# Two weight blocks at a time in the experts' job that mixes two kinds of matmul pass

## The chip, the cores and the metric

One core of a Trainium2 chip runs the whole program. The metric is the device time in microseconds, from launch to end, taken over several runs. The profile is one execution of the same program, recorded by the hardware profiler.

## What is computed

Two layers of a hybrid backbone over 256 latent tokens and 256 context tokens, model width 1024, in float32. Each layer normalises and modulates the stream, projects it into four parallel mixers (pooling, short convolution, neighbourhood attention, state space), projects back, and then applies a feed-forward block. In layer 0 that block is a dense SwiGLU; in layer 1 it is a mixture of experts, and the change touches only that:

```python
logits = (h @ w_router).astype(jnp.float32)
top_v, top_i = lax.top_k(logits, TOP_K)               # 2 of 8 experts for each token
gates = jax.nn.softmax(top_v, axis=-1)
for e in range(N_EXPERTS):
    w_e = jnp.sum(jnp.where(top_i == e, gates, 0.0), axis=-1).astype(h.dtype)
    out = out + w_e[..., None] * swiglu(h, w_gu[e], w_down[e])
# swiglu: g, u = split(h @ w_gu, 2); (silu(g) * u) @ w_down
# w_gu[e] is 1024 x 2816, w_down[e] is 1408 x 1024
```

All weights of all experts are read from device memory once, 138 MB out of the 262 MB that the program reads.

## The kernel before

The kernel is written with a tile framework. Its planner simulates the program and writes out an order of instructions for each engine; each engine then runs its own list strictly in that order, with semaphores between engines. `inorder` adds a dependency without a semaphore: it only tells the planner that one instruction has to stand behind another in the list of the same engine.

**Experts by number of tokens.** The experts are sorted on the chip by how many tokens chose them, so expert 0 is the longest. Each gets a fixed number of token slots. Slots are packed into passes of 128 slots. A *split* pass (128 slots of one expert) multiplies at reduced-precision speed, form `128*128`: ScalarE copies a raw weight block into a high part `wh` (line 284), VectorE subtracts to get the low part `wl` (line 287), and TensorE does three products for each slice of 128 inputs: high by `wh`, high by `wl`, low by `wh`. A *whole* pass multiplies the raw float32 block directly, in quarters of 32 slots, form `128*32`, four of them side by side; it needs no split. Its 128 slots may belong to several experts.

**Jobs.** `moe` runs four jobs one after the other and spreads a fifth one, the last job, between their steps:

- job of expert 0: one pass of a special whole kind, which has its own code (`products2`);
- job of expert 2: one split pass;
- job of experts 1 and 4: a split pass of expert 1 (128 slots), and a whole pass (32 slots of expert 1 and 96 of expert 4). This is the job with two kinds of pass;
- job of expert 3: one split pass;
- the last job, experts 5, 6 and 7: one whole pass. `LAST` names the steps of the other jobs after which one step of it is run. Eleven of these, and one double one, lie in the job of experts 1 and 4; its down half runs at the end of the program.

**One job** (`expert`). The up half has six output blocks `nt`, each of 256 gate and 256 up columns (the sixth has 128 and 128). For each output block the weights come in four blocks of 512 KB for each expert, with two slices `k` of 128 inputs in each; the sixth has two blocks with four slices. For each block, `blocks` loads one raw slot for each expert and splits it if a split pass wants it, and then `products` is called for each pass and each slice. Products accumulate in one PSUM bank for each pass. At the end of an output block comes the gated activation: a tanh on ScalarE, two operations on VectorE (lines 1662 to 1664), and transposes on TensorE (line 1563). The down half has eleven blocks `f` of 512 KB, and each is multiplied for both halves `h` of the output. A job yields after every two blocks, and that is a step: eleven in the up half and five in the down half.

**Buffers.** The raw slots form a ring, which is filled in program order by one DMA queue (SyncE, lines 308 and 323): 15 slots in this stage by the trace, two of them in the tile `xres`. A load waits until the slot's previous block is released. `wh` and `wl` have three buffers each (`NSPLIT`).

**Order of TensorE.** `products` ties each run of a whole pass to the run before it that used the same set of blocks, through `ws["turn"]`. It also notes the latest product of any job in `self.mgu`. Split products are tied to nothing; they run when their `wh` and `wl` are there and the planner puts them there.

Of the kernel before, what the change touches and what calls it, by code (L numbers as in the profile page):

```python
# [247 lines left out]
class Piece:  # L248
# [3 lines left out]
    def __init__(self, col, n, expert, whole, half=None):  # L252
        self.col, self.row, self.n, self.expert, self.whole, self.half = col, col % P, n, expert, whole, half


class Kern:
# [1281 lines left out]
    def expert(self, eids, passes, ys, last=False):  # L1538
# [21 lines left out]
        def trans(pieces, h, j, n):  # L1560
            p = self.ps("m", "atr")
            for i in range(n):
                E.transpose(p[:, i * P:i * P + P], h[:, i * P:i * P + P], self.cst("ident"))
            src = p[:, :n * P].rearrange("p (f s) -> p f s", f=n)
            if pieces[0].whole:
                A.copy(w[:, 0, 2 * j:2 * j + n], src)
                return
            a, = (c.a for c in pieces)
            A.copy(a[:, 0, 2 * j:2 * j + n], src)
            V.tensor_tensor(a[:, 1, 2 * j:2 * j + n], src, a[:, 0, 2 * j:2 * j + n].bitcast(F32), op=OP.subtract)  # L1570

        def trans_sum(p, j, n):

            t = self.tmp("mth")[:, :2 * n * P]
            A.copy(t, p[:, :2 * n * P])
            s = self.stack.shape[-1]
            q = self.ps("m", "atr")
            for i in range(2 * n):
                self.mm(q[:, i * s:i * s + s], t[:, i * P:i * P + P], self.stack)
            gate, up = (q[:, i * n * s:i * n * s + n * s] for i in range(2))  # L1580
            th = self.tmp("mth")[:, :n * s]
            A.activation(th, gate, AF.Tanh, scale=0.5)
            V.scalar_tensor_tensor(th, th, 1.0, gate, op0=OP.add, op1=OP.mult)
            th, up = (v.rearrange("p (f s) -> p f s", f=n) for v in (th, up))
            self.glu = V.scalar_tensor_tensor(w[:, 0, 2 * j:2 * j + n], th, 0.5, up, op0=OP.mult, op1=OP.mult)

        def blocks(gu, *at):
            ws = {}
            for e in eids:
                if gu and self.w0:  # L1590
                    ws[e] = self.w0.pop(0), None
                    continue
                nt, b = at
                if gu:
                    ap = a["mg0"][self.eid[e], nt, b] if nt < 5 else a["mg1"][self.eid[e], b]
                    n, parts = 1024, 1
                elif last:
                    n = min(2, 11 - nt)
                    ap = a["md"][self.eid[e], nt:nt + n, :, b * 512:b * 512 + 512].rearrange("f p c -> p f c")
                    n, parts = n * 512, n  # L1600
                else:
                    ap, n, parts = a["md"][self.eid[e], nt], 1024, 1
                r = self.raw(ap, n, parts, split=parts == 1 or e not in whole)
                ws[e] = r, self.split(r) if e in split else None
            return ws

        def product(out, c, x, w, s, start, stop):
            if c.whole:
                r = w[0]
                if len(r.shape) == 3:  # L1610
                    r, out = r[:, s.start // 256:s.stop // 256], self.quarters(out)
                else:
                    r = r[:, s]
                return [self.mm(out[c.row + q:c.row + q + QUART], x[:, 0, q:q + QUART], r, start=start, stop=stop)
                        for q in range(0, c.n, QUART)]
            wh, wl = (t[:, s] for t in w[1])
            return [self.mm(out, x[:, 0], wh, start=start, stop=False),
                    self.mm(out, x[:, 0], wl, start=False, stop=False),
                    self.mm(out, x[:, 1], wh, start=False, stop=stop)]

        def products(out, pieces, get, ws, s, start, stop):


            ms = [m for c in reversed(pieces) for m in product(out, c, get(c), ws[c.expert], s, start, stop)]
            if pieces[0].whole:
                self.inorder(ws.setdefault("turn", [])[-1:] + ms)
                ws["turn"] = ms
            self.mgu = ms[-1]

        turn = []  # L1630

        def products2(todo):

            ms = [m for t in todo for m in product(*t)]
            self.inorder(turn[-1:] + ms)
            turn[:] = ms
            self.mgu = ms[-1]

        for nt in range(6):
            hw = 256 if nt < 5 else P  # L1640
            kb = 2 if nt < 5 else 4
            ps = [self.ps("g", "mgu") for _ in passes]
            for b in range(8 // kb):
                ws = blocks(True, nt, b)
                for p, (pieces, _) in zip(ps, passes):
                    if half:
                        products2([(p[:, :2 * hw], pieces[kk % 2], pieces[0].x[:, :, b * kb + kk],
                                    ws[pieces[0].expert], slice(kk * 2 * hw, kk * 2 * hw + 2 * hw), b * kb + kk < 2, b * kb + kk > 5)
                                   for kk in range(kb)])
                        continue  # L1650
                    for kk in range(kb):
                        k = b * kb + kk
                        products(p[:, :2 * hw], pieces, lambda c: c.x[:, :, k], ws,
                                 slice(kk * 2 * hw, kk * 2 * hw + 2 * hw), k == 0, k == 7)
                if (last or b % 2) and b < 8 // kb - 1:
                    yield
            for p, (pieces, _) in zip(ps, passes):
                if half:
                    trans_sum(p, nt, hw // P)
                    continue  # L1660
                th = self.tmp("mth")[:, :hw]
                A.activation(th, p[:, :hw], AF.Tanh, scale=0.5)  # L1662
                V.scalar_tensor_tensor(th, th, 1.0, p[:, :hw], op0=OP.add, op1=OP.mult)  # L1663
                self.glu = V.scalar_tensor_tensor(th, th, 0.5, p[:, hw:2 * hw], op0=OP.mult, op1=OP.mult)
                trans(pieces, th, nt, hw // P)
            yield
# [10 lines left out]
        if last:  # L1677
            pieces, gate = passes[0]
            ys += [mp.tile([P, 2, 512], F32R, tag="ymoe", name="ylast", bufs=2),
                   mp.tile([P, 512], F32, tag="aT", name="ylast1", bufs=1)]  # L1680
            for h in range(2):
                p = self.ps("g", "mdn")
                for f in range(11):
                    if f % 2 == 0:
                        ws = blocks(False, f, h)
# [3 lines left out]
                for q in range(2):  # L1689
                    s = slice(q * 256, q * 256 + 256)  # L1690
# [5 lines left out]
                yield  # L1696
            return
        py = [[self.ps("g", "mdn") for h in range(2)] for _ in passes]
        for f in range(11):
            if half:  # L1700
                ws = [blocks(False, f, 0)] if f % 2 == 0 else ws + [blocks(False, f, 0)]
                if f % 2 == 0 and f < 10:
                    continue
                pieces = passes[0][0]
                e = pieces[0].expert
                products2([(py[0][h], pieces[g % 2 if f < 10 else h], pieces[0].a[:, :, g], ws[g % 2][e],
                            slice(h * 512, h * 512 + 512), g < 2, g in ((9, 10), (8, 10))[h])
                           for h in range(2) for g in ((f - 1, f) if f < 10 else (f,))])
                if f % 2:
                    yield  # L1710
                continue
            ws = blocks(False, f, 0)
            for pys, (pieces, _) in zip(py, passes):
                for h in range(2):
                    products(pys[h], pieces, lambda c: c.a[:, :, f], ws, slice(h * 512, h * 512 + 512), f == 0, f == 10)
            if f % 2:
                yield
        for pys, (_, gate) in zip(py, passes):
# [305 lines left out]
```

## Time and profile before

| | us |
|---|---|
| median of 3 runs | 1214.59 (1214.19 to 1215.19) |
| profiled execution, its own time | 1213.07 |
| span of the profile, first to last instruction | 1211.3 |

| engine | busy, us | share of the span |
|---|---|---|
| TensorE, products (PE) | 1165.6 | 96% |
| TensorE, weight loads (PEld) | 831.0 | 69% |
| VectorE (DVE) | 736.8 | 61% |
| ScalarE (ACT) | 461.1 | 38% |

The experts' stage runs from about 830 us to 1200 us of the span. The job of experts 1 and 4 takes about 943 to 1098 us, the job of expert 3 from there to about 1160. In the timeline a product is named by its output and what it reads: `mgu` and `mdn` are the PSUM tiles of the up and down halves, `xg` the tokens of a split pass, `xgv` those of the whole pass of experts 4 and 1, `xgw` those of the last job; `aT`, `aTv` and `aTw` are the same for the down half. A float32 product of form `128*32` is recorded as two instructions, so one block of a whole pass (two slices of four quarters) shows as 16. Products are pipelined and their durations overlap: the distance between two starts is what counts. Shares of the load engines are averages over 16 engines and can read slightly above 1.

### The profile page before, as it was taken

To read this page: it belongs to the slowest core of one execution; us is meant where nothing else is said; L and a number is where in the kernel's file an instruction comes from. 1 tells how busy PE (TensorE), PEld (TensorE's weight loads), DVE (VectorE), ACT (ScalarE), POOL (GpSimd) and SP (SyncE) were. 2 spreads that over 40 slices of the span, in tenths; PEclk is the share of its full clock that TensorE was granted. 3 is DMA by queue.
4 is the path that set the end of the run, shared out by engine and by line. 5 is a ranking of instruction groups with operands and counts; after the bars stand their busy time and mean duration, and the time that the engine had idled before them with its cause. 6 is when DMAs were issued, how large, how long until landed. Compare 5 with 4: busy or idle time off the path is not lost. (4 is left out here: it accounts for less than half of the span.)

```text
span 1211.3 us, 17942 instructions
## 1 busy us (share of the span) xinstructions
PE 1165.6 (96%) x6601; PEld 831.0 (69%) x6601; DVE 736.8 (61%) x1612; ACT 461.1 (38%) x863; POOL 8.9 (1%) x30
## 2 busy tenths in 40 slices
PE   6999999999999999999999999988999999999994
PEld 3787676787788888888886897884467534446741
DVE  4554667347979756764336778644588524447942
ACT  4443453324322231232223555541276423435721
POOL 0000000000000000000000000000000000000000
PEclk9999999999999999999999999998999999999997
DMA  9635424229565443543223442276999999896984
GB/s 373 228 138 209 144 83 139 84 87 374 201 206 187 162 155 128 187 154 122 87 101 126 141 139 88 90 252 244 359 401 407 344 401 394 300 409 238 375 286 179
DMA packets 88752, 264.16 MB, mean 218 GB/s; under 512 B 8144, under 2 KB 24144, under 8 KB 88528
## 3 DMA queue, kind: packets, MB, share of 16 engines
q1 hardware_dynamic: 88080, 260.84, 59.1%
q0 software_dynamic: 576, 2.10, 0.5%
q8 instruction: 54, 0.88, 0.3%
q14 instruction: 42, 0.34, 0.1%
HBM read 261.85 MB, written 1.05 MB: 217 GB/s over the span
## 5 line engine op out<-in xcount | busy, mean ns | idle before, releaser
L287 DVE TENSOR_TENSOR wl<-raw,wh 128x512 fp32r<-128x512 f32 (+2 forms) x288 | 257.0, 920 | 108.9 <-ACT wh L284 108.0
L284 ACT ACTIVATE wh<-raw 128x512 fp32r<-128x512 f32 (+2 forms) x288 | 225.4, 815 | 250.6 <-PE dps L342 67.3
L342 PE MATMUL g<-hmix,wh 128*128 128x512 f32 (+1 forms) x640 | 182.3, 364 | 0.3
L342 PEld LDWEIGHTS g<-hmix,wh 128*128 128x128 f32 x640 | 112.3, 189 | 31.6 <-issue 11.3
L342 PE MATMUL gps<-hffn,wh 128*128 128x512 f32 x320 | 125.0, 394 | 0.8 <-DVE gth L1158 0.8
L342 PE MATMUL ups<-hffn,wh 128*128 128x512 f32 x320 | 124.8, 394 | 0.0
L342 PE MATMUL g<-hmix,wl 128*128 128x512 f32 (+1 forms) x320 | 114.9, 359 | 0.0
L342 PE MATMUL dps<-aT,wh 128*128 128x512 f32 x352 | 111.0, 394 | 0.0
L453 DVE SCALAR_TENSOR_TENSOR sprod<-raw,srep 128x1024 f32<-128x1024 f32 x72 | 87.8, 1220 | 26.3 <-DMA raw<-in_adat_dram 25.8
L342 PE MATMUL mgu<-wh,xg 128*128 128x512 f32 (+1 forms) x288 | 89.2, 381 | 0.0
L342 PEld LDWEIGHTS dps<-aT,wh 128*128 128x128 f32 x352 | 66.0, 188 | 15.8
L342 PEld LDWEIGHTS gps<-hffn,wh 128*128 128x128 f32 x320 | 60.4, 189 | 15.4 <-DVE gth L1158 1.2
L342 PEld LDWEIGHTS ups<-hffn,wh 128*128 128x128 f32 x320 | 60.5, 189 | 14.2
L342 PE MATMUL dps<-aT,wl 128*128 128x512 f32 x176 | 69.7, 396 | 0.0
L342 PEld LDWEIGHTS g<-hmix,wl 128*128 128x128 f32 x320 | 60.4, 189 | 8.4 <-issue 1.0
L342 PE MATMUL ups<-hffn,wl 128*128 128x512 f32 x160 | 63.4, 396 | 0.0
L342 PE MATMUL gps<-hffn,wl 128*128 128x512 f32 x160 | 63.4, 396 | 0.0
L342 PEld LDWEIGHTS mgu<-wh,xg 128*128 128x128 f32 x288 | 52.8, 188 | 13.1 <-issue 3.8
L342 PE MATMUL mgu<-wl,xg 128*128 128x512 f32 (+1 forms) x144 | 57.4, 398 | 0.0
L1138 DVE SCALAR_TENSOR_TENSOR xres<-dps,mods,xres 128x256 f32<-128x256 f32 x64 | 27.5, 477 | 28.6 <-PE dps L342 28.4
L1663 DVE SCALAR_TENSOR_TENSOR mth<-mth,mgu 128x256 f32<-128x256 f32 (+1 forms) x30 | 11.5, 394 | 53.2 <-ACT mth L1662 52.8
L342 PE MATMUL mdn<-wh,aT 128*128 128x512 f32 x132 | 43.5, 400 | 0.0
(396 smaller groups left out, 1820.1 us busy)
## 6 DMA issues: line engine op xcount, KB each, us to landing
raw<-in_mg_dram SPq DMA_DIRECT2D x141, 512.0 KB, 6.7
raw<-in_md_dram SPq DMA_DIRECT2D x76, 512.0 KB, 7.5
raw<-in_ada_dram SPq DMA_DIRECT2D x60, 512.0 KB, 4.1
raw<-in_fg_dram SPq DMA_DIRECT2D x44, 512.0 KB, 4.2
raw<-in_wi_dram SPq DMA_DIRECT2D x40, 512.0 KB, 4.3
raw<-in_adat_dram SPq DMA_DIRECT2D x36, 512.0 KB, 3.3
xres<-in_mg_dram SPq DMA_DIRECT2D x23, 512.0 KB, 7.5
raw<-in_fd_dram SPq DMA_DIRECT2D x22, 512.0 KB, 3.3
```

The source lines that it names most:

```text
L284: up = self.A.activation(h, src, AF.Copy)
L287: sub = self.V.tensor_tensor(lo, src, h.bitcast(F32), op=OP.subtract)
L342: return self.E.matmul(out, l, r, start=start, stop=stop, skip_group_check=True)
L453: V.scalar_tensor_tensor(y, t[:, :1024], 1.0, s[:, j], op0=OP.mult, op1=OP.mult, accum_out=o[:, q, j:j + 1])
L1138: self.V.scalar_tensor_tensor(self.x[:, d, s], ps[:, s], gt[:, j:j + 1], self.x[:, d, s], op0=OP.mult, op1=OP.add)
L1663: V.scalar_tensor_tensor(th, th, 1.0, p[:, :hw], op0=OP.add, op1=OP.mult)
```

## The change

In a job with more than one pass, weight blocks are loaded and split as before, but the products wait for two blocks: first all slices of both blocks for the split pass, then all of both for the whole pass. The same is done in the down half, where the eleventh block is alone. Jobs with one pass keep their order. In addition, a run of a whole pass is no longer tied to the run before it with the same blocks but to the latest product of any job (`self.mgu`), in all jobs that have such runs, the last job included.

```diff
             ms = [m for c in reversed(pieces) for m in product(out, c, get(c), ws[c.expert], s, start, stop)]
             if pieces[0].whole:
-                self.inorder(ws.setdefault("turn", [])[-1:] + ms)
-                ws["turn"] = ms
+                self.inorder([self.mgu] + ms)
             self.mgu = ms[-1]
...
             ps = [self.ps("g", "mgu") for _ in passes]
+            wss = []
             for b in range(8 // kb):
                 ws = blocks(True, nt, b)
-                for p, (pieces, _) in zip(ps, passes):
+                if len(passes) > 1:
+
+                    wss.append(ws)
+                    if b % 2 == 0:
+                        continue
+                    for p, (pieces, _) in zip(ps, passes):
+                        for k in range((b - 1) * kb, (b + 1) * kb):
+                            s = slice(k % kb * 2 * hw, k % kb * 2 * hw + 2 * hw)
+                            products(p[:, :2 * hw], pieces, lambda c: c.x[:, :, k], wss[k // kb], s, k == 0, k == 7)
+                for p, (pieces, _) in zip(ps, passes if len(passes) == 1 else ()):
                     if half:
...
         py = [[self.ps("g", "mdn") for h in range(2)] for _ in passes]
+        wss = []
         for f in range(11):
...
-            ws = blocks(False, f, 0)
+            wss.append(blocks(False, f, 0))
+            if len(passes) > 1 and f % 2 == 0 and f < 10:
+                continue
             for pys, (pieces, _) in zip(py, passes):
-                for h in range(2):
-                    products(pys[h], pieces, lambda c: c.a[:, :, f], ws, slice(h * 512, h * 512 + 512), f == 0, f == 10)
+                for g in range(f - 1 if len(passes) > 1 and f < 10 else f, f + 1):
+                    for h in range(2):
+                        products(pys[h], pieces, lambda c: c.a[:, :, g], wss[g], slice(h * 512, h * 512 + 512), g == 0,
+                                 g == 10)
             if f % 2:
                 yield
```

## Rows read from the trace of the kernel before

**Rows 1.** Chain that ended last, in order of time: start us, us, what.

```profile
1172.47 6.46 DMA raw<-in_md_dram
...
1180.76 10.69 DMA raw<-in_md_dram
```

**Rows 2.** Stages: length; PE, PEld, DVE, ACT, POOL busy (count); clock, DMA share, GB/s.

```profile
943.00:1030.00 87.00, 87.00 (x602) 36.99 (x605) 35.12 (x74) 26.96 (x61) 0.00 (x0) 1.00 1.00 378
1030.00:1098.00 68.00, 68.00 (x463) 28.68 (x455) 29.71 (x56) 26.10 (x54) 0.00 (x0) 1.00 0.92 344
1098.00:1160.00 62.00, 60.03 (x352) 44.46 (x352) 52.63 (x104) 39.44 (x79) 0.00 (x0) 1.00 0.83 297
1160.00:1211.00 51.00, 32.71 (x228) 13.85 (x228) 14.02 (x39) 9.59 (x25) 0.00 (x0) 0.88 0.66 238
```

**Rows 3.** The same columns for two slices of 10 us.

```profile
950.00:960.00 10.00, 10.00 (x72) 4.92 (x74) 4.06 (x8) 1.63 (x3) 0.00 (x0) 1.00 0.77 261
...
1060.00:1070.00 10.00, 10.00 (x67) 4.14 (x66) 5.06 (x8) 3.81 (x7) 0.00 (x0) 1.00 1.03 416
```

**Rows 4.** PE's timeline, experts 1 and 4: start us, us, engine, line, out<-in, form, count.

```profile
942.99 1.92 PE L342 MATMUL mgu<-raw,xgv 128*32 128x512 f32 x16
944.84 0.51 PE L342 MATMUL mgu<-wl,xg 128*128 128x512 f32 x1
...
971.58 1.92 PE L342 MATMUL mgu<-raw,xgw 128*32 128x512 f32 x16
...
1002.57 1.93 PE L342 MATMUL mgu<-xres,xgv 128*32 128x512 f32 x16
1004.43 0.50 PE L342 MATMUL mgu<-wl,xg 128*128 128x512 f32 x1
...
1005.99 1.92 PE L342 MATMUL mgu<-raw,xgv 128*32 128x512 f32 x16
1007.85 0.50 PE L342 MATMUL mgu<-wl,xg 128*128 128x512 f32 x1
...
1008.50 1.92 PE L342 MATMUL mgu<-raw,xgw 128*32 128x512 f32 x16
1010.35 0.50 PE L342 MATMUL mgu<-wh,xg 128*128 128x512 f32 x1
...
1039.36 1.48 PE L342 MATMUL mgu<-raw,xgv 128*32 128x512 f32 x9
...
1042.91 0.44 PE L1563 MATMUL atr<-constp,mth 128*128 128x128 f32 x2
...
1096.92 1.06 PE L342 MATMUL mdn<-rawo,aTv 128*32 128x512 f32 x6
```

**Rows 5.** Waits from 940 to 1060: total us, times, longest us.

```profile
SPq L323 <- PE mgu L342: 56.2, 30, 5.3
...
PEld mgu L342 <- DMA raw<-in_mg_dram: 3.3, 9, 0.4
```

**Rows 6.** One issue on the sync queue; issues by tile, median us to landing, 960 to 1030.

```profile
983.56 2.95 SPq L308 DMA_DIRECT2D xres<-in_mg_dram  x2
...
xres<-in_mg_dram SPq DMA_DIRECT2D x8, 512.0 KB, 7.0
```

**Rows 7.** ACT's timeline at the end of an output block; in brackets idle time before.

```profile
999.20 0.66 ACT L1662 ACTIVATE mth<-mgu 128x256 f32<-128x256 f32 x2 [9.92 <-PE mgu L342]
999.74 1.15 ACT L284 ACTIVATE wh<-xres 128x512 fp32r<-128x512 f32 x2
```

**Rows 8.** Groups of lines, 943 to 1098: busy us, mean ns, idle before.

```profile
L287 DVE TENSOR_TENSOR wl<-raw,wh 128x512 fp32r<-128x512 f32 x55 | 35.3, 686 | 19.6 <-ACT wh L284 19.5
...
L284 ACT ACTIVATE wh<-raw 128x512 fp32r<-128x512 f32 x55 | 31.3, 626 | 16.7 <-PE mdn L342 15.0 <-PE mgu L342 1.8
```

**Rows 9.** Job of expert 3: a wait on PE's timeline; waits from 1100 to 1165.

```profile
1142.70 0.50 PE L342 MATMUL mdn<-wl,aT 128*128 128x512 f32 x1 [1.65 <-DVE wl L287]
...
SPq L323 <- DVE wl L287: 21.6, 13, 4.6
```

## The prediction

> **What bounds the kernel now.** I read the chain of waits first: the program ends on the last expert job's down weights, with two stretches of transfer of 6.46 and 10.69 us in its last 40 us [rows 1]. So what counts is how early the queue of weight loads gets there, and that queue is paced by buffers. Next I read busy time by stage [rows 2]. From 943 to 1098 us runs the job with two kinds of pass (experts 1 and 4). TensorE is busy for all 155 us there, VectorE for 35.12 of 87 and 29.71 of 68. From 1098 to 1160 (expert 3, one split pass) VectorE takes over with 52.63 of 62. In the first of these, the sync queue waits 56.2 us for TensorE to release a weight buffer, while no wait of a weight load of TensorE for a transfer exceeds 0.4 us [rows 5]. A slot loaded at 983.56 takes 7.0 us to land [rows 6] and is multiplied at 1002.57 [rows 4], so it lies ready for some 12 us. I conclude that TensorE's own order sets the pace from 943 to 1098, with transfers close behind: 378 and 344 GB/s in the two halves, where a 10 us slice reaches 416 [rows 2, 3].
>
> **What the change removes.** TensorE's timeline [rows 4] alternates between products of form 128\*128 (split pass) and 128\*32 (whole passes: xgv of this job, xgw of the last job). I price one alternation from its rows. Split stretches: six products from 1004.43 to 1005.99 take 1.56 us, two from 1007.85 to 1008.50 take 0.65; so one costs (1.56-0.65)/4 = 0.23, and a stretch costs 0.65-2\*0.23 = 0.19 besides. Whole stretches: one block's run takes 1.85 us (1008.50 to 1010.35); two runs that happen to be adjacent, 1039.36 to 1042.91, take 3.55, which is 2\*1.85-3.55 = 0.15 less. So an alternation costs 0.34, say 0.35 us.
>
> Their number: from 942.99 to 1096.92 I count 52 stretches of form 128\*32 (the first and last stand in [rows 4]). By the code 33 are blocks of this job's own whole pass (20 + 2 up, 11 down), 12 are blocks of the last job, the rest are runs cut in two. After: 11 up steps with one double run each, and 5 + 1 in the down pass, so 17. The last job's run is now tied behind the latest product, which is the double run's last: it lands next to it, and costs no alternation of its own. At the six ends of an output block the transposes (128\*128) will probably stand between the two, 6 more: 23. Bounds: 17 if all are adjacent, 28 if every last-job run stands alone. Gain (52-23)\*0.35 = 10.2 us, bounds 8.4 and 12.3. No product, load or split is added, and the order of the loads is the same: each step still loads the same blocks in the same turn.
>
> **What it adds: a split pass that needs two split blocks at once.** Three buffers of wh/wl exist. When a pair's split pass begins, its two and the next one are full; the first is released halfway. From there ScalarE and VectorE have the rest of that pass (0.7 us) and the whole runs behind it (3.55 us alone, some 5.2 with the last job's) to refill two. A block costs VectorE 2\*0.686 = 1.37 us and ScalarE 2\*0.626 = 1.25 [rows 8]: 2.7 against 4.2 or more. Inside an output block, and in the down pass, I take 0. At the end of an output block ScalarE's queue is in the way: the tanh of both passes stands ahead of the next split (tanh at 999.20, split at 999.74, [rows 7]), and with it all that is queued behind. Now the tanh of the split pass can run beside the whole run, and only that of the whole pass waits; then follow split 1 (1.25), two copies and split 2. TensorE has the last job's run of 1.85 to cover that, and 1.4 us of the first block's products. I reckon up to 0.7 us open at each of 5 ends, and take 0.2: 1 us, bounds 0 and 3.5.
>
> **At the start of the job** the whole run at 942.99 covered the wait until the first wl at 944.84 [rows 4]. It can't go first any more; the products of the scatter can partly fill in. I take 1 us of the 1.85, bounds 0 and 1.9.
>
> **What stays at nothing, and its cover.** The raw slots of a pair are held until the double run, later than now by up to half a step, and seven are released within some 4 us instead of spread over 9. The cover is the 12 us for which a slot lies ready. A step now takes (1008.50-971.58)/4 = 9.2 us [rows 4] for 7 loads of 0.524 MB, 398 GB/s. With two alternations less it takes 8.5 us, 432 GB/s, which is above 416: the transfers fall behind by 7\*0.524/416 = 8.8 less 8.5, 0.3 us a step, or 3 us in ten steps (6 us at 400 GB/s). That comes out of the 12. From 1030 to 1098 the load engines have 8% free, and before 960 more (261 GB/s) [rows 2, 3], so they catch up. If that cover were gone, the second rival below would hold. The last job's whole runs in the jobs of experts 2 and 3 also lose their freedom: six runs of 1.85 us in stages which VectorE paces; I take 0, bounds -1 and +1.
>
> The Trainium skill would set the ceiling lower. DMA: Bandwidth & Descriptors, "Specifications", states an HBM limit of about 358 GB/s per core. By that rule this stage is at its limit, and the gain is nil. The trace disagrees: 416 GB/s over 10 us [rows 3], and the measurement decides.
>
> **Where the gain goes.** What TensorE saves by 1098 lets the next job begin as much earlier. That job is VectorE's; its queue of loads waits 21.6 us for VectorE's splits [rows 9], and the load engines are used at 0.83, so it keeps its length and moves as a whole. The tail's loads follow from its releases; 297 and 238 GB/s in the two last stages leave room. So the end moves by the whole sum: -10.2+1+1 = -8.2 us. The profiled execution took 1213.07 us (span 1211.3) and becomes 1204.9. The median of the runs is 1.5 us above it, at 1214.59: I predict 1206.5 us. The likeliest case's own range is 1202.5 (12.3 saved, nothing given back) to 1210.5 (8.4 saved, 4.5 given back).
>
> **Rivals.**
> *The transfers bind.* For it: a share of 1.00 in 943 to 1030, and a slot held longer in a ring. Against: 12 us of stock. Then TensorE saves nothing up to 1030, and later at most the 8% of 68 us, 5.4; I reckon half to all of it, 1209 to 1212: 1211 us.
> *The runs don't come together.* The tie only says "after"; the planner that orders each engine may still put the next pair's split products inside a double run or ahead of the last job's run, as it now cuts whole runs in pieces (45 planned, 52 seen). Then some 40 alternations remain: 12\*0.35 = 4.2, less 1 to 2: 1212 us.
> *TensorE starves for splits* (the slower side). Place: the second split block of each of the 17 pairs, with ScalarE's queue held by a tanh or by a wh buffer that TensorE hasn't released. Price: up to a block's 1.37 us each. In the next job such a wait for a wl shows once, 1.65 us [rows 9]. It decides from 10.2/17 = 0.6 us a pair: above that the change loses. At 1.37 it is 17\*1.37 = 23.3 less 10.2: 13 us slower, 1228; at 0.8 it is 1218. Against it: 2.7 us of work in 4.2 or more.
>
> **How the numbers follow.** Forecast 0.58, transfers 0.15, runs apart 0.12, starving 0.15. About 0.2%, 2.4 us, is what a measurement of this kernel can tell from no change: 1212.2 to 1217.0. Faster: all of the forecast, most of the transfers' case and a third of the runs' case, 0.74. The same: what is left of these two and the mildest fifth of starving, 0.14. Slower: 0.12. The range 1202.0 to 1214.5 holds the forecast and the first two rivals, and leaves out the starving and a sliver below.
>
> **What would show it.** In the job's timeline: 17 to 28 stretches of form 128\*32, whole runs of four or six products' rows length (3.55 or 5.2 us), a step of 8.5 us, no idle time ahead of wl products beyond 1 us, and the stage of expert 3 beginning near 1090 instead of 1098. The chain's end would look the same, 8 us earlier. I am wrong if stretches stay above 35, if TensorE shows gaps that end on VectorE's wl or on a transfer of a microsecond or more at most pairs, or if expert 3 begins earlier and the end does not.

## The result, and the profile after

The changed kernel takes 1202.87 us (median of 4 runs, 1199.97 to 1205.38), the kernel before beside it 1214.89 us: a ratio of 0.9898 [0.9877, 0.9918] (the 95% interval stands in brackets here and below), 12.0 us less. On another chip it was 1203.01 against 1214.42, 0.9893 [0.9875, 0.9911]. The profiled execution of the changed kernel took 1202.79 us (span 1201.0), 10.3 us less than that of the kernel before, which had been 1.8 us under its median.

The chain that ended last, in order of time (start us, us, what), after:

```profile
1161.73 6.38 DMA raw<-in_md_dram
1170.06 10.69 DMA raw<-in_md_dram
1180.80 4.57 PE mdn L342 x24
```

The end is the same as in [rows 1]: the last two stretches of transfer, one of 10.69 us again, about 10.7 us earlier. To place the gain I cut both traces at the same events: first split product of experts 1 and 4, first of expert 3, end of expert 3's last wl split, start of the last run (24 recorded instructions of form 128\*32). The columns are those of [rows 2]. Before:

```profile
942.70:1098.70 156.00, 156.00 (x1063) 66.39 (x1062) 65.83 (x129) 54.06 (x116) 0.00 (x0) 1.00 0.96 363
1098.70:1156.70 58.00, 56.04 (x328) 42.67 (x326) 51.91 (x103) 38.30 (x77) 0.00 (x0) 1.00 0.82 296
1156.70:1191.50 34.80, 29.53 (x219) 12.61 (x217) 7.82 (x18) 5.69 (x12) 0.00 (x0) 1.00 0.95 341
```

After:

```profile
943.90:1090.50 146.60, 146.04 (x1066) 69.92 (x1064) 66.21 (x129) 55.36 (x117) 0.00 (x0) 1.00 1.00 379
1090.50:1147.80 57.30, 56.59 (x330) 43.30 (x329) 52.04 (x103) 38.72 (x76) 0.00 (x0) 1.00 0.88 325
1147.80:1180.80 33.00, 28.66 (x219) 12.59 (x217) 7.81 (x18) 5.58 (x12) 0.00 (x0) 1.00 0.98 357
```

In finer numbers: the job starts 1.3 us later (943.93 against 942.66) and takes 146.57 us instead of 156.06 (-9.5), expert 3's job 57.31 instead of 58.01 (-0.7), the tail 32.99 instead of 34.77 (-1.8). With 0.4 us more behind the last run this makes the 10.3 us. The later start is not the work of the new order: 1.3 us are lost already 30 us into the program, where the order on the engines is the same. A second profiled execution of the changed kernel has a job of 146.54 us again, but a tail of 34.01, so a single tail length is good to about a microsecond only. The number of products in a stage and the work of VectorE and ScalarE are the same but for a missing record or two; TensorE does the same job in less busy time.

TensorE's timeline of a step and an end of output block, after, columns as in [rows 4]:

```profile
992.82 0.50 PE L342 MATMUL mgu<-wh,xg 128*128 128x512 f32 x1
...
995.78 3.64 PE L342 MATMUL mgu<-raw,xgv 128*32 128x512 f32 x32
999.35 0.44 PE L1563 MATMUL atr<-constp,mth 128*128 128x128 f32 x2
999.72 1.92 PE L342 MATMUL mgu<-raw,xgw 128*32 128x512 f32 x16
1001.57 0.50 PE L342 MATMUL mgu<-wh,xg 128*128 128x512 f32 x1
...
1004.00 0.50 PE L342 MATMUL mgu<-wl,xg 128*128 128x512 f32 x1 [0.23 <-DVE wl L287]
...
1005.36 1.92 PE L342 MATMUL mgu<-xres,xgv 128*32 128x512 f32 x16
1007.10 1.90 PE L342 MATMUL mgu<-raw,xgv 128*32 128x512 f32 x16
1008.82 1.90 PE L342 MATMUL mgu<-raw,xgw 128*32 128x512 f32 x16
1010.65 0.50 PE L342 MATMUL mgu<-wh,xg 128*128 128x512 f32 x1
```

The whole runs now stand together: two blocks (995.78 to 999.35) or two and the last job's (1005.36 to 1010.65, 5.29 us), with twelve split products ahead (992.82 to 995.78, 2.96 us). A step of two blocks is 2.96 + 5.29 = 8.25 us where it was 9.2. At the end of an output block the transposes come between, as forecast. I count 26 stretches of form 128\*32 in the job, where there were 52.

Waits in the job, after (total us, times, longest us; the sync queue up to 1055, the others up to 1090), and one issue on the sync queue:

```profile
SPq L323 <- PE mgu L342: 49.2, 26, 7.0
...
PE mgu L342 <- DVE wl L287: 0.5, 2, 0.2
...
PEld mgu L342 <- DMA raw<-in_mg_dram: 2.1, 7, 0.4
PEld mdn L342 <- DMA raw<-in_md_dram: 1.3, 4, 0.4
...
ACT wh L284 <- DMA raw<-in_mg_dram: 1.5, 2, 1.1
...
984.94 5.12 SPq L308 DMA_DIRECT2D xres<-in_mg_dram  x2
```

No wait of TensorE for a transfer exceeds 0.4 us, as in [rows 5]; ScalarE's splits wait for one twice, 1.1 us at most. The two loads of the last row, issued at 984.94 and 989.52, land at 994.22 and 995.70 by the trace. ScalarE splits one of the two slots at 1000.09, and TensorE multiplies both raw from 1005.36. So the stock is 10 to 11 us for the whole run and 4 to 6 us for the split. Before, the same two loads (983.56 and 985.97) landed at 991.03 and 992.52, were split at 999.74 [rows 7] and multiplied at 1002.57: 10 to 11.5 us and 7 to 9. The cover of the split has shrunk by some 3 us.

### The profile page after: what moved, and what is told of

Same layout as the page of the kernel before. It is cut to its first block, busy times and chain, and to the rows that moved or that the text cites. A ratio compares the mean times of both kernels' runs of the same rounds, so it can differ in the third digit from the quotient of the medians.

```text
span 1201.0 us, 17945 instructions
## 1 busy us (share of the span) xinstructions
PE 1155.5 (96%) x6601; PEld 835.2 (70%) x6601; DVE 738.2 (61%) x1612; ACT 462.5 (39%) x863; POOL 8.9 (1%) x30
## 4 chain that ended last, share of the span: by engine, by line
PE 90%; DVE 4%; ACT 2%; DMA 2%; issue 1%; SPq 0%; ACTq 0%; DVEq 0%
PE g L342 22%; PE mgu L342 16%; PE dps L342 10%; PE gps L342 9%; PE ups L342 9%; PE mdn L342 7%; PE adaps L342 2%; PE vps L342 2%; PE gath L342 1%; DMA raw<-in_md_dram 1%; PE attS L342 1%; DVE wl L287 1%; PE attO L342 1%; PE scat L342 1%; PE yps L342 1%
## 5 line engine op out<-in xcount | busy, mean ns | idle before, releaser
L342 PE MATMUL ups<-hffn,wl 128*128 128x512 f32 x160 | 63.4, 396 | 0.0
L342 PE MATMUL gps<-hffn,wl 128*128 128x512 f32 x160 | 63.4, 396 | 0.0
L342 PE MATMUL mgu<-raw,xgw 128*32 128x512 f32 (+1 forms) x340 | 44.3, 556 | 0.0
```

The source lines that it names most:

```text
L342: return self.E.matmul(out, l, r, start=start, stop=stop, skip_group_check=True)
```

## The experiments

The theory with which they began (A): an alternation costs 0.35 us, and cutting a whole run inside a group of four products costs more. Where a run is not cut, four products of form 128\*32, one for each quarter of the output, run side by side: in the trace four records start within 0.02 us, and the next four 0.43 us later. Two such fours are a group, since a product is recorded as two instructions. A cut inside a group leaves the other quarters idle. I read it from rows of the kernel before that the forecast had counted as plain alternations. TensorE's timeline in the down pass, before: first a whole group that stands alone, then two neighbouring blocks that are not cut, and one that is:

```profile
1057.07 1.07 PE L342 MATMUL mdn<-raw,aTv 128*32 128x512 f32 x8
1058.06 0.50 PE L342 MATMUL mdn<-wl,aT 128*128 128x512 f32 x1
...
1074.85 1.93 PE L342 MATMUL mdn<-raw,aTv 128*32 128x512 f32 x16
...
1078.30 1.93 PE L342 MATMUL mdn<-raw,aTv 128*32 128x512 f32 x16
...
1085.18 1.92 PE L342 MATMUL mdn<-raw,aTv 128*32 128x512 f32 x14
...
1087.69 1.05 PE L342 MATMUL mdn<-raw,aTv 128*32 128x512 f32 x2
1088.67 0.74 PE L342 MATMUL mdn<-wh,aT 128*128 128x512 f32 x2
```

A block with its split products takes 3.45 us uncut (1074.85 to 1078.30) and 4.63 us cut into 14 and 2 (1085.18 to 1089.81). The product left over (two records) takes 0.98 us to the next start, and a whole group of four (eight records) by itself takes 0.99 (1057.07 to 1058.06): one product costs as much as four. That is 1.2 us for one cut, 0.35 for the alternation and some 0.86 for the group. The rivals: the gain comes from the paired blocks and not from the tie of the runs; it comes from the last job's runs in the tail; transfers or splits limit the new order.

The change has two parts. The *tie* chains each whole run behind the latest product; the *pairing* takes two split passes and then two whole ones. First each alone, and two ways to cut the changed kernel's runs again.

**The tie alone**: the kernel before, with one edit.

```
-                self.inorder(ws.setdefault("turn", [])[-1:] + ms)
-                ws["turn"] = ms
+                self.inorder([self.mgu] + ms)
```

> The kernel before, with one part of the change: a run of whole products is tied behind the latest product of any job; blocks are still taken one at a time. Theory A (TensorE's order in the job of experts 1 and 4 is the whole matter: each stretch of form 128*32 costs 0.35 us, and each run that is cut inside a group of four quarters wastes a slot of 0.86 us besides): the planner's list for TensorE has 41 such stretches there instead of 52, and no run cut inside a group of four, instead of six. So 11*0.35 = 3.9 us and about 4.3 us less: 8 us under the kernel before, some 4 us above the changed kernel. Rival B (only the number of alternations counts, 0.35 each, and cuts cost no more than that): 3.9 us under the kernel before. Rival C (the gain comes from taking two blocks at a time): nothing, within 2.4 us.

Measured: 1203.93 against 1215.09 us, 0.9912 [0.9899, 0.9926]; the job takes 147.91 us, 8.15 less than before, with 41 stretches and none of its runs cut. The theory's sum for that is 11\*0.35 + 4.3 = 8.15 (that it meets the second decimal is luck, as the 0.35 is rounded). The tie alone brings 11 of the 12 us, 3 more than the theory's 8; they lie in the other stages, which the theory did not count (below). The intervals of this kernel and of the changed one overlap, so the times don't show that the pairing adds anything to the tie. The job is 1.3 us shorter with it, in one profile each.

**The pairing alone**: the changed kernel with that edit undone (the two minus lines back).

> The changed kernel with the old tie: two blocks at a time, but a whole run is tied only to the run before it with the same blocks. The planner's list for TensorE then has the same 52 stretches in the job as the kernel before, in the same order. Theory A (TensorE's order is the whole matter): no change, within 2.4 us of the kernel before. Rival C (taking two blocks at a time gains by itself, by what it does to loads and buffers): 4 to 12 us under the kernel before. Rival of my prediction (pairing starves TensorE of splits): above the kernel before by more than 2.4 us.

Measured: 1214.45 against 1215.09 us, 1.0000 [0.9991, 1.0009]; the job takes 156.11 us and has 52 stretches. The order on TensorE is that of the kernel before, product by product: writing the products in pairs changes nothing as long as the planner that orders each engine may place them. So the rival that the pairing makes the gain by itself is out, and the tie is what holds the pairs together.

**Runs cut at the edge of a group, and inside one**: the changed kernel with one split product put in the middle of each pair's whole run, or ahead of its last product. From the edit (`ops[0]` holds a pair's split products, `ops[1]` its whole ones; the second kernel has `n = len(ops[1]) - 1`):

```
...
+            n = len(ops[1]) // 2
+            ms = [m() for m in ops[0][:-1]]
+            first = [m() for m in ops[1][:n]]
+            mid = ops[0][-1]()
+            rest = [m() for m in ops[1][n:]]
+            self.inorder([ms[-1]] + first + [mid] + rest)
+            self.mgu = rest[-1]
...
```

> The changed kernel, with each double run of whole products cut in the middle by the last split product of its pair, by force, at a border between groups of four quarters: 36 stretches of form 128*32 in the job instead of 26, and none cut inside a group (the changed kernel has two). Theory A: 10*0.35 = 3.5 us more for the alternations, 2*0.86 = 1.7 less for the cuts: 1.8 us above the changed kernel, about 10 us under the kernel before. If an alternation cost nothing: 1.7 us under the changed kernel or equal to it. If an alternation cost 1 us: 8 us above it.

> As the clean cut, with the cut put one product before the end of each double run, so inside a group of four quarters: 36 stretches again, 16 runs cut inside a group instead of 2. Theory A (such a cut wastes a slot of 0.86 us, since the one product left over takes as long as four): 3.5 + 14*0.86 = 15.5 us above the changed kernel, 3 us above the kernel before, and 14 us above the clean cut. Rival B (only alternations count): equal to the clean cut within 2.4 us.

Measured: at the edge 1204.09 us, 0.9921 [0.9908, 0.9935], the job 148.60; inside 1218.12 us, 1.0026 [1.0015, 1.0036], the job 161.44. Both lists have 36 stretches; only the place of the cut differs, in 16 pairs. It costs 12.84 us, 0.80 a pair (the theory said 0.86, and half of that for the one pair of the narrow sixth block), and makes a kernel that is slower than the one before. Ten more alternations than in the changed kernel and two cuts fewer cost 2.03 us (theory 10\*0.35 - 2\*0.86 = 1.8). A pair in the second kernel, the same view:

```profile
1082.12 1.89 PE L342 MATMUL mdn<-raw,aTv 128*32 128x512 f32 x14
1083.95 0.50 PE L342 MATMUL mdn<-wh,aT 128*128 128x512 f32 x1
1084.37 1.05 PE L342 MATMUL mdn<-raw,aTv 128*32 128x512 f32 x2
1085.35 0.72 PE L342 MATMUL mdn<-wh,aT 128*128 128x512 f32 x2
```

The one product left over (two records) takes 0.98 us, as in the kernel before. The job of the tie alone, of the cut at the edge and of the cut inside, in the columns of [rows 2]:

```profile
945.30:1093.20 147.90, 147.90 (x1065) 66.99 (x1064) 65.96 (x128) 54.78 (x117) 0.00 (x0) 1.00 1.00 383
```

```profile
943.00:1091.60 148.60, 148.09 (x1065) 68.29 (x1064) 66.25 (x129) 55.42 (x117) 0.00 (x0) 1.00 0.99 377
```

```profile
943.40:1104.80 161.40, 160.95 (x1065) 71.85 (x1063) 66.42 (x129) 55.37 (x117) 0.00 (x0) 1.00 0.94 351
```

VectorE and ScalarE do the same in all three, TensorE shows no idle time to speak of, and the transfers' share goes down as TensorE gets slower. The order of the products is what sets the stage's length.

**The tie in this job's own runs only, and in the last job's runs only** (`last` is true for the last job's pieces in the changed kernel's own code):

```
-                self.inorder([self.mgu] + ms)
+                if last:
+                    self.inorder(ws.setdefault("turn", [])[-1:] + ms)
+                    ws["turn"] = ms
+                else:
+                    self.inorder([self.mgu] + ms)
```

and the same with `if not last`.

> The changed kernel, with the last job's runs on the old tie and only the job of experts 1 and 4 on the new one. The planner's list for TensorE then has the changed kernel's order in that job (26 stretches of form 128*32) and the order of the kernel before at the start of the tail, where the last job's runs meet the scatter and the row products. Theory A (job and tail are two separate gains): the 9.5 us that the job of experts 1 and 4 lost in the changed kernel's profile, and none of some 2 us in the tail: 9.5 us under the kernel before, 2 to 2.5 above the changed kernel. Rival D (the tail got shorter only because the job before it ended earlier and its loads were further ahead): equal to the changed kernel within a microsecond.

> The other half: the changed kernel with the new tie for the last job alone. The planner's list then has the 52 stretches of the kernel before in the job of experts 1 and 4, and the changed kernel's order in the tail. Theory A: only the tail's part, 1.8 to 2.8 us under the kernel before. Rival D: nothing.

Measured: 1204.62 against 1214.90 us, 0.9918 [0.9904, 0.9931], the job 146.04; and 1211.23, 0.9967 [0.9955, 0.9979], the job 156.66. So with the job's own runs tied the kernel gains 10.3 us (8.4 to 11.7 by the interval), and with the last job's runs tied 3.7 (2.6 to 5.5), with 52 stretches in the job as before. That puts rival D out: it said nothing for the second. The two add up to more than the changed kernel's 12.0, but not beyond their intervals. In the profile of the second little of its 3.7 us is seen: its last run waited 3.59 us for a transfer in that execution, and from expert 3's job on it is only 0.7 us faster than the kernel before. TensorE's timeline in the tail, before:

```profile
1156.93 1.92 PE L342 MATMUL mdn<-raw,aTw 128*32 128x512 f32 x16
1158.79 0.50 PE L342 MATMUL mdn<-wl,aT 128*128 128x512 f32 x1
...
1169.91 6.42 PE L342 MATMUL mdn<-raw,aTw 128*32 128x512 f32 x56
...
1191.50 4.48 PE L342 MATMUL mdn<-raw,aTw 128*32 128x512 f32 x24 [2.24 <-DMA raw<-in_md_dram]
```

After:

```profile
1149.01 1.92 PE L342 MATMUL mdn<-raw,aTw 128*32 128x512 f32 x16
...
1159.17 4.50 PE L342 MATMUL mdn<-raw,aTw 128*32 128x512 f32 x40
...
1180.80 4.48 PE L342 MATMUL mdn<-raw,aTw 128*32 128x512 f32 x24 [2.17 <-DMA raw<-in_md_dram]
```

Before, the planner put the last job's first run ahead of expert 3's last split products (the wl at 1158.79), so the scatter behind them and the runs behind that came later: 12.98 us from the first run to the long one (1156.93 to 1169.91), 10.16 after (1149.01 to 1159.17). The other traces settle what of this is the order. The stretch takes 12.97 or 12.98 us in all three kernels that keep the old tie for the last job's runs (before, pairing alone, tie in this job), and 10.13 to 10.16 in all eight executions with the new one and three split buffers. From the end of expert 3's last split to the long run that is 1.8 us less. The same tie shortens expert 2's job by 0.5 us (63.9 to 63.3 or 63.4) and expert 3's by 0.3 to 0.7. Together it is about 3 us in stages that the job's order doesn't touch, which fits the measured 3.7.

From the long run to the last one both take 21.6 us, and both wait some 2.2 us for the transfer. Over these eleven executions this stretch takes 21.3 to 23.3 us, with either tie: there the loads set the pace. That the loads come earlier because their buffers are released earlier is my reading; no run varied it.

**Transposes at the end of a block moved behind the last job's run**, so that the whole runs stand together there too:

```
+            ths = []
...
+                if len(passes) > 1:
+                    ths.append((pieces, th))
+                else:
+                    trans(pieces, th, nt, hw // P)
+            yield
+            for pieces, th in ths:
                 trans(pieces, th, nt, hw // P)
-            yield
```

> The changed kernel with one thing more: in a job with two passes, the transposes at the end of an output block are written behind the yield, so behind the last job's run, which then stands right next to the double run: 21 stretches of form 128*32 instead of 26, the same cuts. Theory A: 5*0.35 = 1.8 us under the changed kernel, 1201. If the transposes' delay holds up the down half or the buffers: at or above the changed kernel.

Measured: 1201.46 against 1214.90 us, 0.9884 [0.9866, 0.9901]; 21 stretches, the job 144.67 us. The job is 1.9 us shorter, as expected for five alternations. Whether the kernel is faster than the changed one can't be told from different chips, so both ran again side by side:

> The changed kernel once more, to stand beside the next one on the same chip: 0.988 to 0.992 of the kernel before.

> The changed kernel with the transposes behind the last job's run, beside the changed kernel on the same chip. Theory A: the job of experts 1 and 4 is 1.8 us shorter and the end comes 1.8 us earlier. If the tail's transfers set the end instead: the job is shorter, and the time is the same within a microsecond.

Measured: 1203.01 us, 0.9893 [0.9875, 0.9911], the job 146.54; and 1202.56, 0.9892 [0.9876, 0.9909], the job 144.65. The job's gain is there again, and the time is the same, where theory A wanted the end 1.8 us earlier. In the profiles the job starts 3.1 us later (946.48 against 943.38), and the section on the hardware shows where that comes from.

**Two split buffers instead of three**: the changed kernel with `NSPLIT = 2`. It leaves the pairs one buffer less to split ahead.

> The changed kernel with two buffers of wh and wl instead of three, to take the cover of the split pass away; the stage of the experts' job with two passes is what is read, since the other jobs lose a buffer as well. My prediction's working (a pair needs 2.7 us of splitting, the rest of the split pass and the whole runs give 4.2 us or more): even two buffers cover it inside an output block and in the down half, so the job of experts 1 and 4 gets longer by 1.7 us for two more cut runs and by up to a block's 1.4 us at each of 5 ends, together 2 to 9 us. The starving rival (a pair's second split comes late): 17 pairs at 1.4, so 20 us or more, with idle time of TensorE that ends on wl at most pairs.

Measured in one execution: 1220.37 us. But the job itself takes 147.69 us, only 1.1 more than with three buffers, and TensorE waits once for a wl, 0.2 us (the timeline's waits from 940 to 1110):

```profile
PE mgu L342 <- DVE wl L287: 0.2, 1, 0.2
```

The job begins at 957.38 instead of 943.93: 13.4 of the 17.6 us between the two profiled executions are lost in the stages before it. The 1.1 us lie under the 2 to 9 expected: two more runs are cut inside a group here, as foreseen, which alone was priced at 1.7, and nothing is seen of a further cost at the ends of the blocks. The mixed job hardly needs the third buffer.

## Why the prediction was right, step by step

The mechanism was right: TensorE's order bounds the job, and fewer changes of form make it shorter. The size was short, 8.2 us forecast and 12.0 measured, and two parts of the gain stood nowhere in the sum: the cut runs (2.6 us) and the last job's runs outside this job (about 3). The result lies 0.9 us above the range's lower end, so that it lies inside is in part luck. The forecast also left open which half of the change does the work: most of it is the tie and not the pairing.

**What bounds the job.** Right. TensorE is busy for 146.04 of 146.60 us, and each experiment that changed its order alone changed the stage's length by the sum worked out for it, within a microsecond. Step 8.25 us (8.5 forecast), expert 3 from 1090.50 (near 1090 forecast).

**The number of alternations.** 26 and not 23, inside the bounds. 26\*0.35 = 9.1 us where I had 10.2.

**The price of an alternation.** It holds, but one of its two parts was read from the wrong rows. The "two runs that happen to be adjacent" at 1039.36 are a cut piece of ten records and a block of 16, not two whole blocks (the x9 in [rows 4] is its start). The piece takes as long as a block because one of its products stands in a group by itself, so the reading came out by luck: two uncut blocks take 3.57 us (995.78 to 999.35), 0.13 less than 2\*1.85 where I had 0.15. What the forecast missed, the price of a cut inside a group, stood in these very rows.

**The price of the cut runs: mis-sized.** "The rest are runs cut in two" were priced at 0.35 us like any other. Twelve ragged pieces (one stands at the end of [rows 4]) come from six runs that were cut inside a group of four, four of them at the price of a whole group and two of half of one: 4.3 us that the sum did not have. The changed kernel keeps two such cuts, 1.7 us, so it gains 2.6 here. The experiments with a cut show this price at 0.80 us a piece.

**The ends of an output block.** I took 0.2 us at each of five and got 0.63 at three, within the bounds of 0 and 3.5. Engine queues at that end, after (ScalarE, then weight load, then TensorE; in brackets idle time before):

```profile
1002.32 0.37 ACT L1566 COPY aTv<-atr 128x256 f32<-128x256 f32 x1 [1.08 <-PE atr L1563]
1002.59 2.19 ACT L284 ACTIVATE wh<-raw 128x512 fp32r<-128x512 f32 x4
...
1003.28 0.19 PEld L342 LDWEIGHTS mgu<-wh,xg 128*128 128x128 f32 x1 [0.27 <-ACT wh L284]
1004.00 0.19 PEld L342 LDWEIGHTS mgu<-wl,xg 128*128 128x128 f32 x1 [0.54 <-DVE wl L287]
```

The chain is the one of the forecast: the second split waits behind a copy on ScalarE, which waits for TensorE's transposes; then TensorE waits for the second wh and wl. Twelve split products and the transposes take 3.79 us there (1001.57 to 1005.36), where twelve alone take 2.96 (992.82 to 995.78). In the kernel with the tie alone, the transposes add 0.20 to six products. That leaves 0.63 us; two other ends, 965.90 to 969.68 and 983.74 to 987.53, take 3.78 and 3.79. At the fourth (1019.42) other products stand between, and no such wait is seen. Three ends make 1.9 us, of which the rows show only a part as idle time, because the ends of products are modelled. This is also why the pairing adds so little to the tie: 41 to 26 stretches should bring 15\*0.35 = 5.25 us, of which 1.7 go to the two cuts and 1.9 to the ends. 1.65 is left, and the two traces differ by 1.34.

**The start of the job.** I took 1 us and find none: products of the job before fill the time until the first wl.

Together: 9.1 + 2.6 - 1.9 = 9.8 us for the job, against 8.2 forecast and 9.5 measured. The 0.3 us between I can't place.

**Expert 3 and the tail.** "It keeps its length and moves as a whole" held within 0.7 us. The last job's runs in the jobs of experts 2 and 3, taken at 0 with a bound of -1, brought 0.5 and 0.7 us, a little past the bound. For its runs at the start of the tail the forecast had no term: "the tail's loads follow from its releases" says nothing of TensorE's order there, which brought 1.8 us. These 3 us are the second part that the sum lacked, and the reason why the whole is nearer to 12 than to 8.

**The range.** Two small slips: 12.3 us saved is 1202.3 and not 1202.5, and the two bounds of what is given back, 3.5 and 1.9, add up to 5.4 and not 4.5. Neither touches the forecast.

**The rivals.** *The transfers bind*: the job moves its bytes at 379 GB/s on average, and no wait of TensorE for a transfer exceeds 0.4 us. The stock was read too high: 12 us was for a slot that ScalarE splits first, and for the split it is 7 to 9 us before and 4 to 6 after, with a wait of 1.1 us for a transfer once. So the cover held, with less to spare than the forecast thought. The experiment with fewer alternations still got faster, to 144.65 us, at 382 GB/s. The limit of about 358 GB/s per core of the Trainium skill (DMA: Bandwidth & Descriptors, "Specifications") is passed here on the average of 147 us. *The runs don't come together*: 26 stretches, so no; but it is what the pairing alone does. *TensorE starves for splits*: dead even with two buffers; its place was right (the ends of a block) and its price, 0.63 us at three places, far from the 17 pairs that it needs.

## What to carry to other kernels

Where an engine's own order bounds a stage, count its changes of form in the timeline, and look at the size of the pieces beside their number: a run cut between groups of side by side products costs 0.35 us here, the same cut inside a group 1.2. Before regrouping work, tie the order that the code has already: the tie of one line brought 11 of 12 us (8 in the job, about 3 in stages that the forecast did not look at), and regrouping without it brought nothing, since a planner put the products back where they were. When two edits come together, run each alone, because the larger idea need not be the one that pays.

## What the hardware showed that was not expected

TensorE's granted clock falls in one stretch in some executions and not in others, though the engine is given the same work. Around 150 us, far ahead of the experts, both profiles of the kernel with the moved transposes and that of the tie alone drop to a granted clock of 0.50 (1.2 GHz). The kernel before and both profiles of the changed kernel keep 1.00 (2.4 GHz). Up to 825 us TensorE, VectorE and ScalarE run the same operations on the same tiles in the same order in all these traces. The kernel with the moved transposes, side by side run, columns as in [rows 2], then TensorE's timeline:

```profile
154.00:156.00 2.00, 2.00 (x7) 1.52 (x6) 2.00 (x8) 0.51 (x2) 0.00 (x0) 0.50 0.00 0
...
148.97 1.12 PE L342 MATMUL attS<-kT,qT 64*128 64x512 f32 x2
150.03 3.04 PE L342 MATMUL yps<-xd,decay 128*128 128x64 f32 x14
...
159.63 0.48 PE L342 MATMUL g<-hmix,wl 128*128 128x512 f32 x1
```

The tie alone, 20 us:

```profile
140.00:160.00 20.00, 20.00 (x95) 15.87 (x95) 10.97 (x33) 9.68 (x24) 1.50 (x4) 0.83 0.25 85
```

The changed kernel on the same chip as the first:

```profile
150.00:160.00 10.00, 10.00 (x58) 7.92 (x58) 5.50 (x25) 4.23 (x13) 0.00 (x0) 1.00 0.16 52
...
150.09 1.12 PE L342 MATMUL attS<-kT,qT 64*128 64x512 f32 x2
151.14 1.77 PE L342 MATMUL yps<-xd,decay 128*128 128x64 f32 x14
...
157.53 0.48 PE L342 MATMUL g<-hmix,wl 128*128 128x512 f32 x1
```

The same 14 products take 3.04 us instead of 1.77, and from them to the wl product at the end 9.60 us (150.03 to 159.63) instead of 6.39 (151.14 to 157.53), 3.2 us more. It had been 1.1 us ahead and is 2.1 us behind from there on, which is most of the 3.1 us by which the experts' job starts later. What the engine did before is short products with few columns in both, and it was busy by the rows throughout.

What decides it stays open, but it is not the kernel alone: the records show both levels within one kernel. Of 23 executions of the kernel before on one chip, eight had a mean granted clock of 0.986 or 0.987 and took 1215.85 to 1216.94 us, fifteen had 0.989 or more and took 1212.30 to 1215.88. A drop as in the rows, some 6 us at half the clock, takes about 0.0025 off the mean of the whole span by my estimate, so these may be the same drop; only profiles tell where the clock fell. With the moved transposes three executions of five had 0.986 (1202.56 to 1203.14 us) and two 0.989 (1199.27 and 1200.06). The changed kernel beside it had two at 0.987 (1203.01 and 1203.71) and three at 0.990 or more (1199.36, 1199.54 and 1203.63). So the drop is as large as what five alternations are worth, and it falls on both. Whether the shorter job would show in the time without it, five executions of each don't tell.
